# Query tiles in the planned order of the input norm and key/value tiles, context chunk first

## The chip, the cores and the metric

The kernel runs on one core of a Trainium2 chip. The metric is the time of one execution on the device in microseconds (us). One profiled execution gives the rows that are shown; its span runs from the first to the last instruction.

Engines by their names in the profile: PE (matrix products), PEld (its weight loads), DVE (vector), ACT (scalar, activations), POOL (GpSimd), SP (which issues nearly all DMAs). Each takes its instructions strictly in the order in which they were written for it; semaphores hold one back until its inputs are there.

## What is computed

One transformer layer over 2048 latent tokens of width 1024, with 256 context tokens ahead of them: a modulated norm, a combined input projection, softmax attention beside a gated delta rule, an output projection, and a gated MLP. What the change touches is the beginning:

```python
sh1, sc1, g1, sh2, sc2, g2 = ada_terms(c, w_mod[l], b_mod[l])
h = modulate(x, norm1_g[l], sh1, sc1)                  # latent tokens
hc = modulate(xc, norm1_g[l], cmod[0], cmod[1])        # context tokens
# of the columns of h @ w_in and hc @ w_in:
kc, vc = attn_kv(ck_a, cv_a, k_norm_g, None)
kl, vl = attn_kv(k_a, v_a, k_norm_g, rope)             # per-head norm, rotary
ql = attn_q(q_a, q_norm_g, rope)
o_attn = block_attention(ql, ...)
...
```

`modulate` is an RMS norm times (1 + scale) plus shift. `attn_q` and `attn_kv` normalise each head of 64, multiply by a gain and rotate by position.

## The kernel before

**The first stage.** The latent tokens come in four chunks of 512 (`x0` to `x3`, 8 tiles of 128x512 each), the context in one of 256 (called -1 in the names). The modulation's two parts are 64 small matmuls (`pm`), whose rows (`mrow`) are transposed into `mps`. A chunk's norm takes squares on ACT (`nsq`), added up on DVE and POOL (`nacc`), a sum over partitions on PE (`nps`), a reciprocal root on POOL (`nrc`), diagonals on DVE (`ndg`), and a matmul that spreads the result (`nrs`). `affine` multiplies each tile by scale and `nrs` on DVE, adds the shift on ACT into `hl..0` (the high part), and puts the rest into `hl..1` (the low part), on POOL for k = 0, 1, 2, 4 and on DVE otherwise. Context tiles are `hc`. High and low parts are kept for all four chunks in `hpool`, since the z projection and the delta rule's projections use them later.

**Key/value and query tiles.** For each 128 tokens `tokproj` makes 24 matmuls (`pq_kv`, 272 columns; `pq_q`, 256 columns, in two halves of four heads each, `q0` and `q1`). `headnorm` squares on ACT (`hsq`), sums on DVE and takes the reciprocal root on POOL (both `hss`), and multiplies on DVE (`hn`). `rope` has two products on POOL (`rb`) and two operations on DVE (`ra`), with a table per chunk (`t12k`, `t12q`) that POOL builds from a DMA. `put` splits into float16 parts (`st`, on ACT and DVE), transposes on PE (`pt`), copies on ACT (`qt`) and stores.

**What sets the order.** `Plan` records the instructions, estimates their durations, and lists them greedily: of those that could start next on an engine, the most urgent by its track's weight goes first. A track of kind "path" is urgent by the length of its remaining chain, one of kind "work" by how much of its PE work is left. The list is then issued as it stands. Before, the list held modulation (`mod`), key/value weights (`w`), norm (`x`) and key/value tiles (`kv`); the context chunk came last:

```python
for i in range(NCH):
    ...
    for k in range(KT):
        affine(i, x[k], rs, hl[i][0][:, k, :], hl[i][1][:, k, :], k)
    ...
x = load_x(-1)
...
plan.issue(dict(mod=("path", 30.0), w=("path", 20.0), kv=("path", KVW), x=("path", 1.0)))
```

The query tiles followed outside the list, through `Direct`, in the order of a loop over halves and tiles, with the transposes of `put` held back by three tiles (`later`, `run_later`); the z projection, also `Direct`, comes next. Weights of the query and z columns, squares, and input tiles that have no other place share the ring `x` of the pool `xp`, of 13 slots. Inputs 0 to 2 were loaded into `hpool` places of later chunks, input 3 into the ring.

Of the kernel before, what the change touches and what calls it, by code (L numbers as in the profile page):

```python
# [10 lines left out]
F32 = mybir.dt.float32  # L11
# [36 lines left out]
XB, LATER, KVW, DTB, PEC = 13, 3, 10.0, 5, 4.0  # L48
# [375 lines left out]

class Direct:
# [14 lines left out]
def kernel(  # L440
# [149 lines left out]
    later = []  # L590

    def run_later(keep):
        while len(later) > keep:
            later.pop(0)()

    def rope_table(e, wk, rows, nm, c, ro, sc):

        t12 = e.tile(wk, [P, 4, 2, 64], F32, "t12", f"t12{nm}{c}", 3)
        e.SY.dma_start(out=t12, in_=rope_d[:, 4 * c:4 * c + 4])
        gv = rows[:, ro:ro + 64]  # L600
        e.G.tensor_tensor(out=t12[:, :, 0, :], in0=t12[:, :, 0, :],
                        in1=gv.unsqueeze(1).broadcast_to([P, 4, 64]), op=ALU.mult)
        for hf in range(2):
            o = slice(32 * hf, 32 * hf + 32)
            oo = slice(32 - 32 * hf, 64 - 32 * hf)
            e.G.tensor_tensor(out=t12[:, :, 1, o], in0=t12[:, :, 1, o],
                            in1=gv[:, oo].unsqueeze(1).broadcast_to([P, 4, 32]), op=ALU.mult)
        if sc != 1.0:
            e.G.tensor_scalar(out=t12, in0=t12, scalar1=sc, scalar2=None, op0=ALU.mult)
        return t12  # L610
# [25 lines left out]
    def put(e, wk, a, nh, nm_, dst):  # L636

        st = e.tile(wk, [P, 4, 2, HD], F16, "st", f"st_{nm_}", 3)[:, :nh]
        e.S.copy(out=st[:, :, 0, :], in_=a)
        e.V.tensor_tensor(out=st[:, :, 1, :], in0=a, in1=st[:, :, 0, :], op=ALU.subtract)  # L640

        def fin():
            pt = e.tile(pst, [P, 1024], F16, "pt", f"pt_{nm_}", 2)
            with e.group():
                for h in range(nh):
                    e.PE.transpose(out=pt[:, h * P:(h + 1) * P], in_=st[:, h].rearrange("p a b -> p (a b)"), identity=id16)
            qt = e.tile(wk, [P, 4, P], F16, "qt16", f"qt_{nm_}", 2)[:, :nh]
            e.S.copy(out=qt, in_=pt[:, :nh * P].rearrange("p (h t) -> p h t", t=P))
            e.SY.dma_start(out=dst, in_=qt)
        later.append(fin)  # L650
        run_later(LATER)

    def front(plan, wk):
# [10 lines left out]
        xs = [place(2, 0, F32, "xs0"), place(3, 0, F32, "xs1"), place(3, 1, F32, "xs2")]  # L664
        hl = [[place(i, f, F32R, f"hl{i}{f}") for f in range(2)] for i in range(NCH)]
        firsts = hl[0] + wms + [xs[0], hl[2][1]] + xs[1:]
# [7 lines left out]
        def load_x(i):  # L674
            ts = []
            for k in range(KT):
                if 0 <= i < NCH - 1:
                    t = xs[i][:, k, :]
                elif i < 0:
# [3 lines left out]
                else:  # L683
                    t = mk(xp, [P, 512], F32, "x", f"x_{i}_{k}", XB)
# [34 lines left out]
        for nb in range(4):  # L719
            if nb == 2:  # L720
                x = load_x(0)
# [11 lines left out]
            row = mk(wk, [2, 512], F32, "qt", f"mrow_{nb}", 2)  # L733
# [4 lines left out]
        rs = stats(0, x)  # L738
# [52 lines left out]

        for i in range(NCH):
# [9 lines left out]
        x = load_x(-1)  # L802
        rs = stats(-1, x)
        hk = []
        for k in range(KT):
            t = mk(xp, [P, 2, TC], F32R, "x", f"hc_{k}", XB)
            affine(-1, x[k], rs, t[:, 0, :], t[:, 1, :], k)
            SY.dma_start(out=hcd[:, :, k, :], in_=t.bitcast(F32))
            hk.append(t)
        for cc in range(NCC):  # L810
            kv_tile(cc, lambda f, k, cc=cc: hk[k][:, f, cc * P:(cc + 1) * P], None)

        plan.track = "kv"
        run_later(0)
        plan.track = "x"
# [5 lines left out]
        return [[t.get() for t in h] for h in hl], ab.get(), rows.get(), gm.get(), sil.get(), [t.get() for t in wq]  # L821

    with tc.tile_pool(name="wk", bufs=2, reuse_waits="tile") as wk:
        hl, ab, rows, gm, sil, ws = front(Plan(tc, ps1, pst, psn), wk)


        direct = Direct(nc)

        def of_chunk(tt):
            sl = slice((tt % 4) * P, (tt % 4 + 1) * P)  # L830
            return lambda f, k: hl[tt // 4][f][:, k, sl]

        for hf in range(2):
            for tt in range(NTT):
                n_ = f"q{hf}_{tt}"
                if tt % 4 == 0:
                    t12 = rope_table(direct, wk, rows, f"q{hf}", tt // 4, R_Q, 0.125)
                ps = tokproj(direct, of_chunk(tt), ws, 256, n_)
                y = headnorm(direct, wk, ps[:, :256], 4, n_)
                a = rope(direct, wk, y, 4, tt % 4, t12, n_)  # L840
                put(direct, wk, a, 4, n_, qsc[tt, :, 4 * hf:4 * hf + 4, :])
            ws = load_w(direct, wiz[0] if hf else wiq[1], f"qz{hf}")
        run_later(0)
# [1587 lines left out]
```

## Time and profile before

| | |
|---|---|
| median of 3 runs | 3209.25 us |
| lowest, highest | 3205.55, 3211.18 us |
| the profiled execution | 3206.93 us |
| its span | 3205.2 us, mean granted PE clock 0.975 |
| busy over the span | PE 3049.6 (95%), PEld 1954.9 (61%), DVE 2387.5 (74%), ACT 1769.9 (55%), POOL 1532.4 (48%) |

PE's busy time counts matmuls that overlap and run slower at a low granted clock, so that 95% is no measure of what PE could do. Shares over the whole span mix stages with different limits; the stage in question is the first 268 us.

### The profile page before, as it was taken

To read this page: it belongs to the slowest core of one execution; us is meant where nothing else is said; L and a number is where in the kernel's file an instruction comes from. 1 tells how busy PE (TensorE), PEld (TensorE's weight loads), DVE (VectorE), ACT (ScalarE), POOL (GpSimd) and SP (SyncE) were. 2 spreads that over 40 slices of the span, in tenths; PEclk is the share of its full clock that TensorE was granted. 3 is DMA by queue.
4 is the path that set the end of the run, shared out by engine and by line. 5 is a ranking of instruction groups with operands and counts; after the bars stand their busy time and mean duration, and the time that the engine had idled before them with its cause. 6 is when DMAs were issued, how large, how long until landed. Compare 5 with 4: busy or idle time off the path is not lost.

```text
span 3205.2 us, 62953 instructions
## 1 busy us (share of the span) xinstructions
PE 3049.6 (95%) x25298; PEld 1954.9 (61%) x25298; DVE 2387.5 (74%) x3669; ACT 1769.9 (55%) x2876; POOL 1532.4 (48%) x1241
## 2 busy tenths in 40 slices
PE   6899999987999999999997999899999999999998
PEld 2789978874667777777775554344444444444445
DVE  5766487877777777788885778877777777976676
ACT  5534134445777777777776545555555555544332
POOL 4786365555887777777777434322333223000000
PEclk8899999997999999999998999999999999999999
DMA  6222334562112222233323565322222222696696
GB/s 246 86 77 82 113 128 127 168 177 81 49 42 76 67 78 84 93 117 110 104 96 114 216 236 187 122 92 99 92 99 99 93 96 79 204 309 203 218 311 216
DMA packets 287333, 423.63 MB, mean 132 GB/s; under 512 B 22984, under 2 KB 166952, under 8 KB 285744
## 3 DMA queue, kind: packets, MB, share of 16 engines
q1 hardware_dynamic: 285088, 414.19, 39.0%
q0 software_dynamic: 1952, 5.42, 0.6%
q8 instruction: 198, 3.24, 0.4%
q14 instruction: 95, 0.78, 0.1%
HBM read 284.15 MB, written 135.81 MB: 131 GB/s over the span
## 4 chain that ended last, share of the span: by engine, by line
PE 76%; DVE 10%; POOL 5%; DMA 3%; issue 3%; ACT 3%; SPq 0%; POOLq 0%; DVEq 0%; ACTq 0%
PE pdn L422 12%; PE ub L422 10%; PE sc L422 7%; PE uc L422 7%; PE ua L422 6%; PE ops L422 6%; PE po L422 6%; PE sm L422 3%; PE pa L422 2%; PE pg L547 1%; PE pg L546 1%; PE pg L548 1%; PE pw L422 1%; DVE mx L422 1%; PE pz L422 1%
## 5 line engine op out<-in xcount | busy, mean ns | idle before, releaser
L422 POOL TENSOR_TENSOR lp<-p,hp 128x1024 f16<-128x1024 f32 x288 | 620.0, 2160 | 208.5 <-DVE hp L422 84.0
L422 PEld LDWEIGHTS <-ws_u 128*128 128x128 f16 x3696 | 361.1, 98 | 444.4 <-issue 20.6
L422 DVE TENSOR_REDUCE mx<-sm 128x2 f32<-128x1024 f32 (+1 forms) x320 | 356.5, 1114 | 95.2 <-PE sm L422 92.3
L422 PE MATMUL pdn<-hid,wd 128*128 128x512 f16 (+1 forms) x1980 | 400.8, 365 | 0.0
L422 ACT ACTIVATE p<-sc 128x1024 f32<-128x1024 f32 x288 | 295.0, 1024 | 127.3 <-PE sc L422 123.6
L422 PEld LDWEIGHTS <-wd 128*128 128x128 f16 x1980 | 193.8, 98 | 204.7
L422 DVE SCALAR_TENSOR_TENSOR cv<-xa,ufw,cv 128x1025 f32<-128x1025 f32 (+1 forms) x176 | 254.9, 1501 | 48.8 <-ACT cv L422 48.7
L422 POOL TENSOR_TENSOR ws_u<-raw_u,ws_u 128x512 f16<-128x512 f32 x110 | 176.4, 1615 | 138.4 <-ACT ws_u L422 114.6
L422 PE MATMUL sc<-q,kh 128*128 128x512 f16 x576 | 220.4, 383 | 6.3 <-ACT p L422 5.9
L422 PE MATMUL sc<-qx,kx 128*128 128x512 f16 x576 | 220.1, 382 | 0.0
L422 POOL TENSOR_TENSOR nrc_f<-nrc_f,mhalf 128x8 f32<-128x8 f32 x3 | 5.5, 1837 | 424.1 <-DVE nrc_f L422 424.1
L422 ACT CAST hp<-p 128x1024 f16<-128x1024 f32 x192 | 201.0, 1047 | 3.7
L422 PE MATMUL ops<-vst,hp 128*128 128x65 f16 (+1 forms) x4608 | 191.9, 193 | 1.3 <-ACT hp L422 1.1
L422 PE MATMUL ua<-blk_a,ws_u 128*128 128x512 f16 x792 | 181.7, 379 | 1.9 <-ACT s L422 1.9
L422 PEld LDWEIGHTS <-hp 128*128 128x128 f16 x4608 | 164.9, 97 | 21.0 <-issue 7.1
L422 PE MATMUL po<-ol,ws_o 128*128 128x512 f16 x768 | 174.9, 385 | 0.1
L546 PE MATMUL pg<-hl,ws_g 128*128 128x512 f32 x384 | 152.7, 398 | 0.0
L548 PE MATMUL pg<-hl,ws_g 128*128 128x512 f32 x384 | 152.3, 397 | 0.0
L547 PE MATMUL pg<-hl,ws_g 128*128 128x512 f32 x384 | 151.7, 395 | 0.0
L422 POOL TENSOR_TENSOR usg<-usg,mhalf 128x3 f32<-128x3 f32 x22 | 19.1, 867 | 276.8 <-DVE usg L422 276.8
L422 ACT CAST t<-pa 128x512 f16<-128x512 f32 x216 | 124.5, 583 | 44.2 <-PE pa L422 40.3
L422 PE MATMUL sm<-kh,q 64*128 64x512 f16 (+1 forms) x320 | 119.0, 372 | 18.5 <-DVE mx L422 18.3
(704 smaller groups left out, 7779.3 us busy)
## 6 DMA issues: line engine op xcount, KB each, us to landing
rd<-in_wd SPq DMA_DIRECT2D x70, 512.0 KB
hid<-hidc SPq DMA_DIRECT2D x70, 512.0 KB
raw_u<-in_wu SPq DMA_DIRECT2D x44, 512.0 KB
tk<-gsc SPq DMA_DIRECT2D x34, 512.0 KB
tT<-gsc SPq DMA_DIRECT2D x66, 256.0 KB
hidc<-cv SPq DMA_DIRECT2D x22, 768.0 KB
wm<-in_wm SPq DMA_DIRECT2D x64, 256.0 KB
gsc<-kd SPq DMA_DIRECT2D x64, 256.0 KB
```

Source lines behind the costliest of these rows:

```text
L422: fn(**{k: v.get() if isinstance(v, Lazy) else v for k, v in kw.items()})
L546: PE.matmul(out=ps, lhsT=hi_l(k), rhs=hi_r(k), start=st, stop=False)
L547: PE.matmul(out=ps, lhsT=hi_l(k), rhs=lo_r(k), start=False, stop=False)
L548: PE.matmul(out=ps, lhsT=lo_l(k), rhs=hi_r(k), start=False, stop=en)
```

## The change

The query tiles become part of the planned list, as a track `q` of kind "work" with weight 0.5; key/value tiles become "work" with weight 2. The context chunk is normed first, then the four latent chunks. After each latent chunk's key/value tiles the list records that chunk's tiles of the first query half; the second half follows. The transposes of `put` are recorded at once, and the planner places them. Inputs 0, 2 and 3 land, tile by tile, in the places of their chunk's low parts (`places`, `Pieces`), and the affine's product goes to a ring tile `xm`. Input 1 lands where chunk 3's high part will be. The rope tables of keys and queries get rings of two each. The plan's fixed costs per instruction and its factor for DVE and POOL side by side (`fixed`, `PORT`) are set to the values that a later stage uses.

```diff
-XB, LATER, KVW, DTB, PEC = 13, 3, 10.0, 5, 4.0
+XB, QW, DTB, PEC = 13, 0.5, 5, 4.0
...
+class Pieces:
+    def __init__(self, tiles):
+        self.tiles = tiles
+    def __getitem__(self, idx):
+        return self.tiles[idx[1]][idx[0], idx[2]]
...
-        t12 = e.tile(wk, [P, 4, 2, 64], F32, "t12", f"t12{nm}{c}", 3)
+        t12 = e.tile(wk, [P, 4, 2, 64], F32, f"t12{nm[0]}", f"t12{nm}{c}", 2)
...
-        later.append(fin)
-        run_later(LATER)
+        fin()
...
-        xs = [place(2, 0, F32, "xs0"), place(3, 0, F32, "xs1"), place(3, 1, F32, "xs2")]
-        hl = [[place(i, f, F32R, f"hl{i}{f}") for f in range(2)] for i in range(NCH)]
+        def places(i, f, dtype, name):
+            return Pieces([mk(hpool, [P, 512], dtype, f"h{i}{f}{k}", f"{name}_{k}", 1) for k in range(KT)])
+        xs = [place(3, 0, F32, "xs1") if i == 1 else places(i, 1, F32, f"xs{i}") for i in range(NCH)]
+        hl = [[places(i, f, F32R, f"hl{i}{f}") if f and i != 1 else place(i, f, F32R, f"hl{i}{f}") for f in range(2)]
+              for i in range(NCH)]
...
-            V.scalar_tensor_tensor(out=x, in0=x, scalar=aff1[:, k, b:b + 1], in1=rs, op0=ALU.mult, op1=ALU.mult)
+            if i >= 0:
+                raw, x = x, mk(xp, [P, 512], F32, "x", f"xm_{i}_{k}", XB)
+            else:
+                raw = x
+            V.scalar_tensor_tensor(out=x, in0=raw, scalar=aff1[:, k, b:b + 1], in1=rs, op0=ALU.mult, op1=ALU.mult)
...
             if nb == 2:
-                x = load_x(0)
+                x = load_x(-1)
+            if nb == 3:
+                x0 = load_x(0)
...
-        rs = stats(0, x)
+        rs = stats(-1, x)
...
+        xn, hk = x0, []
+        for k in range(KT):
+            t = mk(xp, [P, 2, TC], F32R, "x", f"hc_{k}", XB)
+            affine(-1, x[k], rs, t[:, 0, :], t[:, 1, :], k)
...
+        x, rs = xn, stats(0, xn)
...
+        for cc in range(NCC):
+            kv_tile(cc, lambda f, k, cc=cc: hk[k][:, f, cc * P:(cc + 1) * P], None)
+        def q_tiles(hf, i, ws):
+            plan.track = "q"
+            t12 = rope_table(plan, wk, rows, f"q{hf}", i, R_Q, 0.125)
+            for tt in range(4 * i, 4 * i + 4):
+                n_ = f"q{hf}_{tt}"
+                ps = tokproj(plan, of_chunk(tt), ws, 256, n_)
+                y = headnorm(plan, wk, ps[:, :256], 4, n_)
+                a = rope(plan, wk, y, 4, tt % 4, t12, n_)
+                put(plan, wk, a, 4, n_, qsc[tt, :, 4 * hf:4 * hf + 4, :])
...
-        x = load_x(-1)
-        rs = stats(-1, x)
...
-        wq = load_w(plan, wiq[0], "q0")
-        plan.keep(wq)
+            if i == 0:
+                wq = load_w(plan, wiq[0], "q0")
+            q_tiles(0, i, wq)
+        wq = load_w(plan, wiq[1], "q1")
+        for i in range(NCH):
+            q_tiles(1, i, wq)
+        wz = load_w(plan, wiz[0], "z0")
+        plan.keep(wz)
...
-        plan.issue(dict(mod=("path", 30.0), w=("path", 20.0), kv=("path", KVW), x=("path", 1.0)))
+        plan.issue(dict(mod=("path", 30.0), w=("path", 20.0), kv=("work", 2.0), x=("path", 1.0), q=("work", QW)))
...
+        plan.fixed, plan.PORT = (150, 60, 0, 140, 42), 0.58
```

Before, PE has no query matmul ahead of the last key/value tile. The loops of the query and z tiles outside the list are gone for the queries and unchanged for z.

How the order moves, at three places. First ACT's rows around the last modulation row `mrow_3`. Before:

```order
L422 ACTIVATE nsq_a0_7_240<-xs0_122 128x512
L422 CAST ws_kv0_265<-raw_kv0_186 128x272
...
L422 COPY mrow_2_301<-pm_2_247 2x512
L422 ACTIVATE nacc_a1_307<-xs1_124 128x512
L422 COPY mrow_3_314<-pm_3_251 2x512
L422 ACTIVATE nsq_a1_1_320<-xs1_124 128x512
```

After:

```order
L422 ACTIVATE nacc_a-1_281<-xc_0_194 128x256
L422 COPY mrow_2_286<-pm_2_268 2x512
L422 CAST ws_kv0_290<-raw_kv0_211 128x272
...
L422 COPY mrow_3_307<-pm_3_271 2x512
L422 ACTIVATE nsq_a-1_1_311<-xc_0_194 128x256
```

Chunk 0's squares stood ahead of `mrow_3`, with those of chunk 1 behind it; now the context's squares but the first stand behind it, and chunk 0's behind those.

Second, POOL's rows where the first query tile stands. Before, behind the last key/value tiles (kv0 and kv1 are the context's):

```order
L422 TENSOR_TENSOR hss_kv1_1584<-hss_kv1_1584,mhalf_80 128x2
L601 TENSOR_TENSOR t12q02_2031<-t12q02_2031,rows_205 128x4x64
L606 TENSOR_TENSOR t12q02_2031<-t12q02_2031,rows_205 128x4x32 x2
L609 TENSOR_SCALAR t12q02_2031<-t12q02_2031 128x512
L496 TENSOR_SCALAR hss_q0_0_1676<-hss_q0_0_1676 128x4
L497 TENSOR_TENSOR hss_q0_0_1676<-hss_q0_0_1676,mhalf_80 128x4
```

After, among the key tables of chunk 2 and chunk 1's low parts (`hl11`):

```order
L422 TENSOR_TENSOR rb_kv5_882<-hn_kv5_870,t12k0_262 128x2x32 x2
L422 TENSOR_TENSOR t12k2_892<-t12k2_892,rows_224 128x4x64
L422 TENSOR_SCALAR hss_q0_0_940<-hss_q0_0_940 128x4
L422 TENSOR_TENSOR t12k2_892<-t12k2_892,rows_224 128x4x32
L422 TENSOR_TENSOR hss_q0_0_940<-hss_q0_0_940,mhalf_80 128x4
L422 TENSOR_TENSOR t12k2_892<-t12k2_892,rows_224 128x4x32
L422 TENSOR_SCALAR hss_q0_1_976<-hss_q0_1_976 128x4
L422 TENSOR_TENSOR hl11_992<-xm_1_0_886,hl10_903 128x512
```

The query tiles have moved from behind the norm into it.

Third, SP's loads. Before, the first query weights stand behind nearly all key/value stores and the context's stores (`hcd`):

```order
L422 DMA raw_q00_1523<-in_wiq 128x512
L422 DMA hcd_72<-hc_5_1504 256x1x256
...
L422 DMA ksc_62<-qt_kv17_1572 128x256
L422 DMA raw_q02_1582<-in_wiq 128x512
L599 DMA t12q02_2031<-in_rope 128x512
```

After, the rope tables stand behind the last input tile, and the query weights right behind the context's key/value stores:

```order
L422 DMA xs3_7_146<-in_xt 128x512
L422 DMA t12q00_258<-in_rope 128x512
L422 DMA t12q01_260<-in_rope 128x512
L422 DMA t12k0_262<-in_rope 128x512
...
L422 DMA vsc_63<-vs_kv1_556 128x128
L422 DMA raw_q00_589<-in_wiq 128x512
L422 DMA ksc_62<-qt_kv0_611 128x256
```

Tables moved behind all inputs, query weights ahead of the latent key/value tiles.

More of the change, by code (lines that the diff above doesn't have):

```diff
@@ L422, in issue, with get @@
                     fn(**{k: v.get() if isinstance(v, Lazy) else v for k, v in kw.items()})
+class Pieces:
[3 more added lines that the diff above has]
+        return self.tiles[idx[1]][idx[0], idx[2]]
+    def get(self):
+        return Pieces([t.get() for t in self.tiles])
 class Direct:
@@ L588, in tokproj @@
         return ps
[L590 to L594, printed above, removed]
     def rope_table(e, wk, rows, nm, c, ro, sc):
-        t12 = e.tile(wk, [P, 4, 2, 64], F32, "t12", f"t12{nm}{c}", 3)
+        t12 = e.tile(wk, [P, 4, 2, 64], F32, f"t12{nm[0]}", f"t12{nm}{c}", 2)
         e.SY.dma_start(out=t12, in_=rope_d[:, 4 * c:4 * c + 4])
@@ L663, in front @@
         wms = [place(1, f, F32, f"wms{f}") for f in range(2)]
-        xs = [place(2, 0, F32, "xs0"), place(3, 0, F32, "xs1"), place(3, 1, F32, "xs2")]
-        hl = [[place(i, f, F32R, f"hl{i}{f}") for f in range(2)] for i in range(NCH)]
-        firsts = hl[0] + wms + [xs[0], hl[2][1]] + xs[1:]
+        def places(i, f, dtype, name):
[3 more added lines that the diff above has]
+              for i in range(NCH)]
+        firsts = [hl[0][0]] + xs[0].tiles + wms + [hl[2][0]] + xs[2].tiles + [xs[1]] + xs[3].tiles
         ab = once(const, [P, NCK, 16], F32, "ab")
@@ L705, in affine @@
             hf = hi.bitcast(F32)
-            V.scalar_tensor_tensor(out=x, in0=x, scalar=aff1[:, k, b:b + 1], in1=rs, op0=ALU.mult, op1=ALU.mult)
+            if i >= 0:
+                raw, x = x, mk(xp, [P, 512], F32, "x", f"xm_{i}_{k}", XB)
+            else:
+                raw = x
+            V.scalar_tensor_tensor(out=x, in0=raw, scalar=aff1[:, k, b:b + 1], in1=rs, op0=ALU.mult, op1=ALU.mult)
             S.activation(out=hi, in_=x, func=AF.Identity, bias=mod1[:, k, b:b + 1])
@@ L732, in front @@
                               start=kp + k == 0, stop=kp + k == KT // 2)
-            row = mk(wk, [2, 512], F32, "qt", f"mrow_{nb}", 2)
+            row = mk(xp, [2, 512], F32, "x", f"mrow_{nb}", XB)
             S.copy(out=row, in_=pm[:2, :])
@@ L790, in of_chunk @@
             return lambda f, k: hl[i][f][:, k, sl]
+        xn, hk = x0, []
+        for k in range(KT):
+            t = mk(xp, [P, 2, TC], F32R, "x", f"hc_{k}", XB)
+            affine(-1, x[k], rs, t[:, 0, :], t[:, 1, :], k)
+            SY.dma_start(out=hcd[:, :, k, :], in_=t.bitcast(F32))
+            hk.append(t)
+        plan.track = "mod"
+        x, rs = xn, stats(0, xn)
+        plan.track = "x"
+        for cc in range(NCC):
[9 more added lines that the diff above has]
+                put(plan, wk, a, 4, n_, qsc[tt, :, 4 * hf:4 * hf + 4, :])
+            plan.track = "x"
         for i in range(NCH):
@@ L801, in front @@
                 kv_tile(NCC + 4 * i + j, of_chunk(4 * i + j), t12)
-        x = load_x(-1)
-        rs = stats(-1, x)
[L804 to L813, printed above, removed]
@@ L821, in front @@
-        return [[t.get() for t in h] for h in hl], ab.get(), rows.get(), gm.get(), sil.get(), [t.get() for t in wq]
+        plan.issue(dict(mod=("path", 30.0), w=("path", 20.0), kv=("work", 2.0), x=("path", 1.0), q=("work", QW)))
+        return [[t.get() for t in h] for h in hl], ab.get(), rows.get(), gm.get(), sil.get(), [t.get() for t in wz]
     with tc.tile_pool(name="wk", bufs=2, reuse_waits="tile") as wk:
-        hl, ab, rows, gm, sil, ws = front(Plan(tc, ps1, pst, psn), wk)
-        direct = Direct(nc)
@@ L829, in of_chunk @@
[L829 to L842, printed above, removed]
@@ L843, with of_chunk @@
-        run_later(0)
+        plan = Plan(tc, ps1, pst, psn)
+        plan.fixed, plan.PORT = (150, 60, 0, 140, 42), 0.58
+        hl, ab, rows, gm, sil, ws = front(plan, wk)
+    direct = Direct(nc)
+    def of_chunk(tt):
+        sl = slice((tt % 4) * P, (tt % 4 + 1) * P)
+        return lambda f, k: hl[tt // 4][f][:, k, sl]
     def decay_setup():
```

6 lines of the change are left out of this document (removed).

## The prediction

> **What bounds the kernel now.** The change touches the first stage alone, up to the point where the z projection starts, so I read that stage: first the busy times by stretch, then which tile opens the z stage, then who waits for whom, then the groups of the engine that is waited for. The stretches (time, length, then PE, PEld, DVE, ACT, POOL busy, the granted clock, the DMA share):
>
> ```profile
> core 0: us, PE busy (x) PEld busy (x) DVE busy (x) ACT busy (x) POOL busy (x), PEclk, DMA share, GB/s
> 0.00:44.00 44.00, 33.10 (x90) 7.84 (x90) 10.62 (x32) 13.37 (x26) 7.13 (x10) 1.00 0.96 339
> 44.00:100.00 56.00, 34.17 (x187) 29.20 (x188) 50.08 (x83) 39.15 (x83) 45.34 (x49) 0.72 0.32 110
> 100.00:154.00 54.00, 44.22 (x315) 40.93 (x314) 37.37 (x96) 28.16 (x93) 40.98 (x75) 0.91 0.27 78
> 154.00:170.00 16.00, 11.43 (x76) 10.55 (x76) 6.61 (x19) 5.89 (x19) 5.31 (x8) 0.89 0.51 147
> 170.00:214.00 44.00, 42.62 (x363) 41.76 (x364) 29.26 (x69) 16.36 (x39) 38.39 (x64) 0.96 0.22 63
> 214.00:268.00 54.00, 50.51 (x447) 49.11 (x446) 35.59 (x87) 22.90 (x56) 46.66 (x76) 1.00 0.22 69
> 268.00:321.50 53.50, 51.25 (x426) 50.63 (x425) 35.63 (x100) 24.99 (x47) 26.83 (x29) 0.97 0.31 98
> ...
> L585 PE MATMUL pq_z<-ws_qz,hl x128: 276/282/415, 268.3 to 321.3; 128*128 128x256 f32 x128
> ```
>
> The second row group says where the stage ends: the first z matmul starts at 268.3 us. Up to 268, POOL is busy 7.13 + 45.34 + 40.98 + 5.31 + 38.39 + 46.66 = 183.8 us, and 176.7 of the 224 us after 44 (79%). DVE has 158.9 of those 224 (71%), PE 183 (82%, but with stretched matmuls at a clock of 0.72 to 0.94). No engine is full over the whole, but each part has its own limit. From 44 to 100 (norm and key/value tiles) DVE is at 89% and POOL at 81%. From 100 to 154 nobody is over 82%. From 154 to 170 everything is half idle. From 170 on (query tiles) POOL is at (38.39 + 46.66)/98 = 87%. The waits, and two pieces of the chain that ended last, name the reasons:
>
> ```profile
> DVE hn_q L621 <- POOL hss_q L497: 10.9, 19, 1.6
> POOL t12q L601 <- DMA t12q<-in_rope: 10.7, 7, 5.0
> DVE ra_q L633 <- POOL rb_q L629: 9.5, 15, 1.6
> ...
> PE pq_q L585 <- DVE hn_q L621: 6.7, 6, 2.4
> PE pq_q L585 <- ACT ws_q L422: 4.5, 3, 2.0
> ...
> 154.63 4.09 DMA raw_q<-in_wiq
> 159.58 3.40 DMA raw_q<-in_wiq
> ```
>
> PE waits for `hn_q` (a PSUM buffer that DVE frees), which waits for POOL's `hss_q`: the query tiles go at POOL's pace. Around 160 the query weights have not come: two DMAs of 4.09 and 3.40 us are the chain. POOL's groups up to 275 us:
>
> ```profile
> L497 POOL TENSOR_TENSOR hss_q<-hss_q,mhalf 128x4 f32<-128x4 f32 x32 | 33.5, 1047 | 2.3
> L629 POOL TENSOR_TENSOR rb_q<-hn_q,t12q 128x128 f32<-128x128 f32 x64 | 32.0, 519 | 6.9 <-DVE hn_q L621 4.3 <-DVE ra_q L633 2.6
> ...
> L609 POOL TENSOR_SCALAR t12q<-t12q 128x512 f32<-128x512 f32 x8 | 12.4, 1554 | 0.6
> ...
> L496 POOL TENSOR_SCALAR hss_q<-hss_q 128x4 f32<-128x4 f32 x32 | 10.3, 322 | 8.1 <-DVE hss_q L618 5.5
> L606 POOL TENSOR_TENSOR t12q<-t12q,rows 128x128 f32<-128x128 f32 x16 | 8.7, 565 | 0.0
> ...
> L601 POOL TENSOR_TENSOR t12q<-t12q,rows 128x256 f32<-128x256 f32 x8 | 6.2, 772 | 10.7 <-DMA t12q<-in_rope 10.7
> ```
>
> The 32 query tiles cost POOL 33.5 + 32.0 + 12.4 + 10.3 + 8.7 + 6.2 = 103.1 us, 3.2 a tile. The change removes no part of it: POOL's rows stand in another order, but there are as many.
>
> **The change part by part.** The yardstick is therefore POOL's work against its share of the time. The new end of the stage is: the time at which the mixed work starts, plus POOL's work from there, divided by the share that it reaches.
>
> *Context first.* Before, the first latent chunk's sums were squared under the modulation matmuls, and its affine began right when the modulation was there. Now ACT has `mrow_3` ahead of the context's squares, so the sums start after it. The rows of before: when `mrow_3` and the affine came, and what the context's sums (`nacc_a-1`, with its four small matmuls), its rstd column (`nrc`, with two `ndg`) and its spread matmul cost, each filtered by its tile in a window:
>
> ```profile
> 40.73 0.56 ACT L422 COPY mrow<-pm 2x512 f32<-2x512 f32 x1
> 42.89 1.13 DVE L422 TENSOR_TENSOR aff<-aff,cols 128x16 f32<-128x16 f32 x1
> 44.05 2.72 DVE L422 SCALAR_TENSOR_TENSOR xs<-xs,aff,nrs_a 128x512 f32<-128x512 f32 x4
> ...
> 94.00:125.00 31.00, 0.67 (x4) 0.60 (x4) 1.95 (x4) 0.44 (x1) 2.26 (x3) 0.87 0.17 48
> ...
> 120.00:140.00 20.00, 0.72 (x3) 1.01 (x1) 0.83 0.17 47
> ...
> 120.00:140.00 20.00, 0.65 (x2) 0.30 (x2) 0.57 (x2) 0.83 0.17 47
> ```
>
> `mrow_3` ends at 40.73 + 0.56 = 41.3. One square of 0.4, then the chain of adds 1.95 + 2.26 = 4.2, the matmuls 0.67, rstd and diagonal 0.72 + 1.01 = 1.7, the spread 0.65: 48.6, where 44.05 stood. I take 48.5 (between 47, should handovers overlap, and 51, should each cost more). By then POOL has done 2.26 + 1.01 = 3.3 us instead of 7.13, so 183.8 - 3.3 = 180.5 us are left. The context's affine itself is not new, only earlier.
>
> *Inputs in the place of their low parts.* The same 32 multiplies write a ring tile instead of their own input, and as many DMAs go out: no instruction is added. Chunks 2 and 3 are now asked for at once, and the rope tables stand behind them on SP. Ahead of the tables are 16 loads of 512 KB, 24 + 8 of 256 KB (the latter by the rows below), the context (1 MB), key/value weights and rows (1.5 MB): 19.3 MB.
>
> ```profile
> wms<-in_wm SPq DMA_DIRECT2D x16, 512.0 KB
> xs<-in_xt SPq DMA_DIRECT2D x24, 256.0 KB
> x<-in_xt SPq DMA_DIRECT2D x8, 256.0 KB
> ```
>
> At the 339 GB/s of the first row that is 57 us; had all the time the best rate, it would be some 50. POOL comes to the tables at about 52, after the first chunk's sums: a wait of 0 to 5 us, I take 2. In return the later inputs (0.6 us of waiting now) and the query tables (10.7 us of POOL's waiting, the row above) are there early.
>
> *Query tiles in the plan.* POOL's holes are the gain: 56 + 54 - 86.3 = 23.7 us from 44 to 154, 10.7 from 154 to 170, 13 from 170 to 268. In the new order `hss_q`, `rb_q` and the tables stand between the norm's subtractions, and `raw_q00` stands ahead of the second key/value tiles, so the hole at 154 should go entirely. What share is reached? The first part (five affines, kv 0 to 13, q0_0 to q0_6) has both DVE and POOL heavily loaded; its bound from below is the 79% of POOL from 44 to 154, its best witness the 89% of DVE from 44 to 100. The second part (25 query tiles, four kv tiles) is like today's 170 to 268, 87%. I take 88% for the whole: 180.5/0.88 = 205.1.
>
> *The weights between halves, and the z stage.* The load of the second query half and of z stands in the same ring of 13; today's change of halves shows no stall at 214 (PE 50.51 of 54). From z on the code is the same; I cost it at nothing. Its cover is the PE work of 51.25 in 53.5 us; if late z weights broke it, the price is that of today's first weights, 16 - 11.43 = 4.6 us.
>
> **Sum.** 48.5 + 2 + 205.1 = 255.6, where 268.3 stood: -12.7 us. The profiled execution took 3206.93 us (span 3205.2), so 3194.2; the median of the runs shown, 3209.25, is 2.3 above it: 3196.5, said as 3196.
>
> PE does not forbid it:
>
> ```profile
> 250.00:268.00 18.00, 18.00 (x164) 17.73 (x162) 11.91 (x31) 7.87 (x19) 14.23 (x24) 1.00 0.15 49
> ```
>
> Here PE is full with 164 matmuls in 18 us, 0.11 each. The 432 of key/value, 768 of query and 164 transposes are 150 us, less than 205; PE would be at 73%.
>
> **The rivals.** *Port contention takes a good part back.* DVE and POOL lengthen each other when both stream from memory; the same four diagonals took 0.88 us with POOL idle and 4.42 beside POOL's sums and subtractions of 1.27 us each, and the subtractions of chunk 3 stretched too:
>
> ```profile
> 39.05 0.88 DVE L422 TENSOR_SCALAR ndg_a<-k,nrc_a 128x128 f32<-128x128 f32 x4
> 57.60 4.42 DVE L422 TENSOR_SCALAR ndg_a<-k,nrc_a 128x128 f32<-128x128 f32 x4 [0.72 <-POOL nrc_a L422]
> 57.54 1.27 POOL L422 TENSOR_TENSOR nacc_a<-nacc_a,nsq_a 128x512 f32<-128x512 f32 x1
> ...
> L422 DVE SCALAR_TENSOR_TENSOR hl<-x,mod,hl x4: 740/1420/1749, 120.2 to 124.0; 128x512 fp32r<-128x512 f32 x4
> L422 POOL TENSOR_TENSOR hl<-x,hl x4: 1252/1297/1803, 115.2 to 124.0; 128x512 fp32r<-128x512 f32 x4
> ```
>
> The Trainium skill, GPSIMD Engine Reference, section Specifications, says that GpSimd's memory interfaces are shared with VectorE and contend with its instructions that have two tensor inputs or run in a two-port mode. The trace agrees with these rows, and by that rule a denser mix costs more per instruction. Its price here: if 36 affine operations of three chunks stretch like the four (1.42 for 0.74), DVE gains 36 x 0.68 = 24 us, to 158.9 + 24 = 183; at the 89% that is its best, 206, which alone changes nothing; POOL's two-input work of some 45 us stretching by a tenth adds 4.5/0.88 = 5, and uneven queues behind stretched instructions about as much: stage end 262 to 265, time 3203 to 3206.
>
> *PE-like packing.* The planner's order fits, POOL reaches 95%: 50.5 + 190 = 240.5, time 3181. For it speaks that 32 independent tiles now fill any hole; against it that no stretch above shows POOL over 87%.
>
> *Slower: the in-order queues keep POOL at the share of the planned stage.* Every engine takes its rows in the planned order, and the planned part of today reached 86.3/110 = 78% although the order was planned too. Query and key/value tiles share one `rb`, two `hn`, and five free slots of the ring of 13 while eight hold query weights; one late row holds up all behind it. At 78%: 50.5 + 231 = 282, time 3223. It decides from a share of 180.5/(268.3 - 50.5) = 83% downwards; there the late start is no longer earned back.
>
> *The change does nothing measurable:* the share lies at 82 to 86%, between today's planned and query parts, so that the filled holes pay only for the late start; stage end 260 to 270, time 3199 to 3209.
>
> **How the numbers follow.** Forecast (share 86 to 91%) 0.40, contention 0.17, close packing 0.15, nothing measurable 0.10, slower 0.18. The range holds shares from 81% (50.5 + 223 = 273.5, time 3214) to 95.5% (3180). Measurement tells 0.2%, 6.4 us, from no change: faster means under 3202.8, slower over 3215.7. Forecast and packing are faster (0.55); contention straddles 3203, two fifths of it faster (0.07) and three fifths the same (0.10), with all of the case of nothing (0.10); of the slower rival two thirds lie beyond 3215.7 (0.12), the rest within (0.06). That gives 0.62 faster, 0.26 same, 0.12 slower.
>
> **What would show it.** The first z matmul at about 255 instead of 268.3; POOL at 86 to 91% from 50 to there; the first context affine at 48 to 49; no wait for `raw_q` and none of several us for the rope tables; from the first z matmul to the end the same 2937 us. I am wrong if POOL's operations get longer by over a tenth, if DVE or ACT shows waits for ring tiles (`xm`, `rb`, `hn`) in the first part, if PE starves at either change of weights, or if the z stage lasts longer.

## The result, and the profile after

The changed kernel takes 3226.9 us (median of 4 runs, 3221.8 to 3228.9) where the kernel before takes 3209.7 in the same runs: ratio 1.0052, interval [1.004, 1.0065]. It is slower by 17 us. Forecast were 3196 us and a gain of 13; the sign was wrong, and the time lies above the range.

The profiled execution has a span of 3225.7 us (3205.2 before). The same stretches as before (time, length, busy times of PE, PEld, DVE, ACT, POOL with counts, granted clock, DMA share, GB/s), and the row that ends the stage:

```profile
0.00:44.00 44.00, 31.25 (x80) 6.74 (x80) 6.63 (x23) 10.40 (x23) 1.75 (x7) 0.97 0.95 341
44.00:100.00 56.00, 38.46 (x183) 32.60 (x184) 40.26 (x78) 28.94 (x74) 37.23 (x47) 0.66 0.49 168
100.00:154.00 54.00, 45.36 (x307) 41.15 (x305) 37.98 (x80) 30.96 (x71) 41.99 (x61) 0.87 0.14 40
154.00:170.00 16.00, 11.47 (x60) 9.96 (x61) 14.14 (x22) 7.37 (x19) 14.29 (x17) 0.68 0.06 17
170.00:214.00 44.00, 38.28 (x313) 36.84 (x312) 31.92 (x77) 22.48 (x58) 33.87 (x55) 0.96 0.21 62
214.00:268.00 54.00, 49.82 (x428) 47.79 (x427) 33.56 (x83) 22.20 (x59) 46.28 (x76) 1.00 0.25 75
...
188.00:281.40 93.40, 84.90 (x721) 82.37 (x722) 60.67 (x152) 39.09 (x104) 78.30 (x130) 0.98 0.24 72
```

```profile
L598 PE MATMUL pq_z<-ws_z,hl x256: 277/281/420, 281.4 to 383.4; 128*128 128x256 f32 x128
```

The first z matmul comes at 281.4 us instead of 268.3: 13.1 of the 20.4 us by which the last matmul is later (3212.3 against 3191.9) arise in the stage that was changed. The hole from 154 to 170 is gone, as intended: POOL has 14.29 us of 16 there, 5.31 before. But up to 100 us POOL has done 39.0 us of work where it had done 52.5. Both stages whole, as one row each (before, then after):

```profile
0.00:268.30 268.30, 216.36 (x1479) 179.65 (x1479) 169.82 (x384) 125.96 (x315) 184.03 (x279) 0.91 0.39 127
```

```profile
0.00:281.40 281.40, 227.49 (x1479) 187.72 (x1480) 173.54 (x384) 128.06 (x315) 186.12 (x279) 0.88 0.36 122
```

The instructions are as many (1479, 384, 315, 279), POOL's busy time grew by 2 us, and PE needs 11.1 us more for the same 1479 matmul records, at a granted clock of 0.88 instead of 0.91. DVE's, ACT's and POOL's busy times grew by 2 to 4 us; for the rest of the 13 us these three wait. Pieces of the chain that ended last, from the changed kernel (pieces called issue, of less than 0.1 us each, are left out): the start, and a stretch in which query tiles stand between the norm's subtractions:

```profile
35.10 4.78 DMA rows<-in_rows
39.90 0.22 DVE gm L422
...
47.44 1.86 DVE ws_kv L422 x2
49.30 1.41 DVE ndg_a-1_379 L422 x2
50.76 1.24 PE nrs_a-1_383 L422 x2
52.02 0.87 DVE xc L422 x2
...
111.06 0.98 POOL hss_q L422
112.06 0.43 DVE hn_q L422
112.53 0.43 POOL hss_q L422
113.04 1.33 POOL hl L422
114.37 0.42 POOL rb_q L422
114.79 0.97 POOL hss_q L422
```

At the start the context's affine (`xc`) comes at 52.0. In the second stretch read the starts: from one `hss_q` power to the next 3.73 us pass (111.06 to 114.79). Within them a query tile's `hn_q` can only follow its own power; then come the next tile's scaling (112.53), a subtraction of 1.33 us and an `rb_q`, and only behind these two the next tile's power. POOL is nearly full in this stretch (4.84 us of the 5 from 110 to 115), so it shows who stands behind whom, and not where POOL's idle time lies. The waits from 44 us to the stage's end (us in total, times, longest):

```profile
...
DVE hn_q L422 <- POOL hss_q L422: 20.1, 24, 2.5
...
POOL hss_kv L422 <- DVE hss_kv L422: 10.6, 5, 8.3
...
PE pq_kv L422 <- DVE hn_q L422: 6.5, 4, 4.9
POOL t12k L422 <- DMA t12k<-in_rope: 6.3, 2, 3.2
```

`hn_q` waits 20.1 us for POOL where it waited 10.9 before. POOL's own longest wait, 8.3 us up to 93.15, is of another kind: it waits for the sum of a key/value tile, and the chain there is mostly key/value matmuls, at a granted clock of 0.55 from 85 to 90 us:

```profile
85.41 5.21 PE pq_kv L422 x25
90.62 0.12 PE nps_a L422 x2
90.73 1.63 PE pq_kv L422 x12
```

### The profile page after: what moved, and what is told of

It is laid out like the page before. It is cut to its first block, busy times and chain, and to the rows that moved or that the text cites. A ratio compares the mean times of both kernels' runs of the same rounds, so it can differ in the third digit from the quotient of the medians.

```text
span 3225.7 us, 62936 instructions
## 1 busy us (share of the span) xinstructions
PE 3061.8 (95%) x25298; PEld 1964.2 (61%) x25298; DVE 2392.6 (74%) x3669; ACT 1772.0 (55%) x2876; POOL 1532.9 (48%) x1241
## 4 chain that ended last, share of the span: by engine, by line
PE 75%; DVE 10%; POOL 5%; issue 4%; DMA 3%; ACT 3%; SPq 0%; POOLq 0%; DVEq 0%; ACTq 0%
PE pdn L422 12%; PE ub L422 10%; PE sc L422 7%; PE uc L422 7%; PE ua L422 6%; PE ops L422 6%; PE po L422 6%; PE sm L422 3%; PE pa L422 2%; DVE mx L422 1%; DMA wm<-in_wm 1%; PE pw L422 1%; PE pg L560 1%; PE pg L559 1%; PE pg L561 1%
```

## The experiments

Each with the median, the ratio to the kernel before in the same runs (which took 3209.65 to 3211.93) and the first z matmul of the profiled execution. That last figure is of one execution; in `early_il` (3229.5 us) and `interleave` (3230.5) it was the longest of the runs, some 9 and 4 us above the median:

| kernel | us | ratio [interval] | first z |
|---|---|---|---|
| changed | 3226.9 | 1.0052 [1.004, 1.0065] | 281.4 |
| ctx_last | 3239.9 | 1.0088 [1.007, 1.0106] | 295.0 |
| q_outside | 3233.7 | 1.0072 [1.0055, 1.0089] | 290.8 |
| both_back | 3251.3 | 1.0124 [1.0109, 1.0139] | 305.1 |
| old_costs | 3226.5 | 1.0046 [1.0031, 1.0061] | 281.8 |
| stats_track | 3231.6 | 1.0063 [1.0047, 1.008] | 285.1 |
| before_places | 3225.4 | 1.0047 [1.0032, 1.0062] | 284.9 |
| before_places_track | 3219.5 | 1.0028 [1.0019, 1.0038] | 280.0 |
| kv_path | 3230.9 | 1.0061 [1.0046, 1.0076] | 283.1 |
| interleave | 3226.6 | 1.0047 [1.0033, 1.0062] | 280.1 |
| early_il | 3220.9 | 1.0034 [1.0021, 1.0047] | 282.0 |
| before_places_il | 3233.5 | 1.0068 [1.0051, 1.0084] | 292.3 |
| before_kv | 3217.4 | 1.0016 [1.0007, 1.0026] | 271.9 |
| warm | 3230.4 | 1.0054 [1.0039, 1.0069] | 284.8 |
| before_warm | 3214.5 | 1.0009 [0.9999, 1.0018] | 273.9 |
| less_pe | 3224.1 | 1.0042 [1.0027, 1.0056] | 275.0 |
| less_pool | 3214.1 | 1.001 [1.0001, 1.0019] | 269.1 |
| before_scale | 3204.2 | 0.9974 [0.9962, 0.9985] | 261.0 |
| early_scale | 3213.8 | 1.0007 [0.9998, 1.0015] | 266.4 |

**Which part loses? Parts taken back one at a time.** `ctx_last` loads and computes the context after the last chunk again:

```
-            if nb == 2:  x = load_x(-1)
-            if nb == 3:  x0 = load_x(0)
+            if nb == 2:  x = load_x(0)
...
+        x = load_x(-1); rs = stats(-1, x); ...      # behind the chunks
         wq = load_w(plan, wiq[1], "q1")
```

> The changed kernel with the context chunk normed last again (chunk 0's sums under the modulation, as before); query tiles stay in the planned list, inputs and planner costs stay as changed. Theory A (the context-first order is the loss: the first latent affine came at 65.95 us instead of 44.05, and the work behind it was not denser): the first latent affine is back at 44 to 46 and the first z matmul comes at 262 to 268, time 3203 to 3212. Theory B (the mixing of query tiles into the norm is the loss, the start is made up for): first z matmul at 278 or later, time over 3221.

`q_outside` takes the query tiles out of the planned list:

```
-            q_tiles(0, i, wq)
...
+        for hf in range(2):
+            for tt in range(NTT): ...               # directly, as before
```

> The changed kernel with the query tiles behind the planned list again, as before (with their held-back transposes); context first, inputs and planner costs as changed. Theory A: the late start stays and nothing fills the holes, so the first z matmul comes at 280 or later, time 3222 to 3235. Theory B: the norm runs undisturbed, the stage ends at 270 to 275, time 3210 to 3216.

`both_back` does both, so that of the change only the inputs' places with the product tile `xm`, the modulation rows in ring x, the planner's numbers, the key/value track's weight and transposes, and the two rings of rope tables are left:

> Context last and query tiles outside: only the inputs' places (with the ring tile of the affine's product) and the planner's costs and key/value weight are as changed. Theories A and B both: within 4 us of the kernel before, 3206 to 3214, first z matmul 266 to 272. A rival (the places or the costs are the loss): 3220 or more.

`old_costs` is the changed kernel with the planner's numbers of before (`plan.fixed` and `plan.PORT` not set):

> The changed kernel with the planner's fixed costs and its factor for DVE beside POOL as before; all else changed. A and B: 3221 to 3232, the costs move single rows only. Rival C (the new cost values make a worse list): 3215 or less.

Theory A fails in `ctx_last`, B in `q_outside`, both in `both_back`, and C in `old_costs` (the numbers of B in `ctx_last` and of A in `q_outside` did come, but neither theory has both); what came in `both_back` is the rival, that the places or the costs are the loss (3220 or more). Undoing the context's place or the query tiles' makes it slower, so each of these two named parts is a gain: from `both_back` 17.6 us for the context, 11.4 for the query tiles, 24.4 for both. The planner's numbers do nothing in the changed kernel that can be told. What loses is the rest: `both_back` stands 41 us behind the kernel before.

**The inputs' places and the turns in ring x.** A ring's buffers are given in the order of recording within a track. The squares of chunk i+1 (`nsq_a`) and the eight products of chunk i (`xm`) now stand in ring x on one track, the squares behind the products. The squares in before, and after:

```profile
L422 ACT ACTIVATE nsq_a<-xs x21: 612/614/631, 18.3 to 53.7; 128x512 f32<-128x512 f32 x21
L422 ACT ACTIVATE nsq_a<-x x7: 627/630/633, 61.3 to 78.9; 128x512 f32<-128x512 f32 x7
```

```profile
L422 ACT ACTIVATE nsq_a<-xs x28: 612/629/655, 41.6 to 162.9; 128x512 f32<-128x512 f32 x28
```

The last square came at 78.9 and now comes at 162.9, ahead of chunk 3's affine. That it costs time was the next theory (D). Four kernels: `stats_track` (the changed kernel, squares and sums of chunks 1 to 3 on a track of their own, `n`, of kind "path" with weight 1),

```
         def stats(i, x):
+            was = plan.track
+            if i > 0: plan.track = "n"
...
+            plan.track = was
```

> The changed kernel with one thing undone in effect: the statistics of chunks 1 to 3 are recorded on a track of their own, so that their squares need not take their turn in ring x behind the eight product tiles (xm) that the affine now allocates there. Nothing else changes. Theory D (the products' new ring tiles hold the next chunk's squares back, so that each chunk's chain becomes serial): chunk 1's squares start at 41 to 55 us instead of 71, chunk 3's rstd comes by 125 instead of 177.5 us, first z matmul at 250 to 266 us instead of 281.4, time 3194 to 3212 against 3226.9. Rival E (the weight of the key/value track, work 2.0, is the loss): first z within 3 us of 281, time 3222 to 3230. Rival F (the inputs' pieces or the separate rope-table ring land late): the same as E.

`before_places` (the kernel before with the places and `xm` alone: the lines on `xs`, `hl`, `firsts` and the multiply of the diff above),

> The kernel before with one part of the change alone: inputs land in tiles of their own where the low parts go, and the affine writes a product tile in ring x instead of working in place. Context last, query tiles outside, weights, costs and rope-table ring as before. Theory D: the chunks' chain becomes serial, first z at 283 to 300 us against 268.3, time 3224 to 3243. Rivals E and F in its rope-table form: nothing of theirs is in this kernel, so 3206 to 3213. F in its pieces form: slower as in D, and no better in the next run.

`before_places_track` (the two edits together),

> The kernel before with the inputs' places and product tiles, as in the run ahead of it, and the statistics of chunks 1 to 3 on a track of their own. Theory D: back to about the kernel before, first z 262 to 275 us, 3203 to 3216. F in its pieces form: within 5 us of the run ahead of it.

and `kv_path`:

```
-kv=("work", 2.0)
+kv=("path", 10.0)
```

> The changed kernel with the key/value track's weight put back from work 2.0 to path 10.0; the rings' turns stay. Rival E: first z at 260 to 270 us and 3205 to 3214. Theory D: chunk 3's rstd stays after 165 us, first z at 278 to 290, time 3222 to 3236.

The places with the product tile alone cost 14.7 us (3225.4 against 3210.7), though they add no instruction; that is shown. Theory D holds for a part at most: with the own track the kernel before gets 5.9 of them back, which the intervals hardly tell apart, and the changed kernel nothing. In the latter the last square comes at 79.9 instead of 162.9, but the products come late:

```profile
L422 DVE SCALAR_TENSOR_TENSOR xm<-xs,aff,nrs_a x32: 730/737/748, 85.2 to 155.3; 128x512 f32<-128x512 f32 x32
```

The first starts at 85.2 us (65.9 in the changed kernel), the last at 155.3 (186.3): on a track of their own the sums of chunks 1 and 2 ran ahead of the first products, and DVE did them first. So in this kernel early squares did not bring the stage's end forward (285.1 against 281.4). In `before_places` a single wait at the change to the query tiles has grown too (5.5 us before):

```profile
POOL hss_q L509 <- DVE hss_q L631: 12.2, 1, 12.2
```

The weight (`kv_path`) is not the loss: 3230.9.

**The turns again, with nothing else moved.** `interleave` records square and sum k of the next chunk right behind affine k, on the same track:

```
+            by = stats_by(i + 1, xn)
             for k in range(KT):
                 affine(i, x[k], rs, ...)
+                rn = next(by, None)
-                x, rs = xn, stats(i + 1, xn)
```

> The changed kernel with one order of recording altered: square and sum k of the next chunk are recorded right after affine k of this one, on the same track, instead of after all eight. No weight, place or instruction differs; only the turns in ring x do. Theory D2 (the turns behind the products cost, and an own track fails because it lets the squares run ahead of the context's products as well): first z at 262 to 275 us instead of 281.4, time 3206 to 3220 against 3226.9. Rival G (the turns are harmless; the loss is the late start by 100 us and then POOL's share in the mixed order, which is PE, DVE and POOL waiting for each other's short tiles): first z within 4 us of 281, 3221 to 3232.

`early_il` also records the context's sums ahead of `mrow_3`:

```
             if nb == 3:
                 x0 = load_x(0)
+                rs = stats(-1, x)
```

> As the run ahead of it, and the context's squares and sums are recorded ahead of the fourth row of the modulation (mrow_3), so that they don't take their ring turn behind it. Theory D2: the first context affine comes at 44 to 47 us instead of 52.0, and the stage ends 4 to 8 us before that of the run ahead of it: 3200 to 3214. Rival G: the same gain of 4 to 8 us, but from 281: 3218 to 3226. If the early start is eaten by a later wait: no difference to the run ahead of it.

`before_places_il` is `before_places` with the same interleaving:

> The kernel before with the inputs' places and product tiles (3225.4), and the squares of the next chunk recorded between the affines of this one. Theory D2: 3207 to 3216 and first z at 266 to 276 us instead of 284.9. Rival G: 3221 to 3230.

`before_kv` is the kernel before with the weight and the transposes of the change alone:

```
-        later.append(fin); run_later(LATER)
+        fin()                                       # in the plan
-kv=("path", KVW)
+kv=("work", 2.0)
```

> The kernel before with two small parts of the change alone: the key/value track's weight is work 2.0 instead of path 10.0, and the transposes of a planned key/value tile are recorded with it instead of three tiles later. Places, context and query tiles as before. Theory D2: these parts cost little by themselves, 3205 to 3216. Rival E2 (they are the 26 us that lie between the kernel with the places alone, 3225.4, and the one with context and query tiles back, 3251.3): 3225 to 3240, first z at 283 to 298 us.

Interleaving gives nothing in the changed kernel (3226.6) and loses 8 us in `before_places`. It is a weak test of theory D, since in these two kernels the last square moved little (from 162.9 to 156.2, and from 109.7 to 105.9); with the own track, where the squares did come early, the stage still ended at 285.1 and 280.0. So D is not borne out as the main cause. `before_kv` costs 6 us, so of the 26 us between `before_places` and `both_back` that part is small. If the parts add up, 14.7 of the 41 us go with the places, 6 with the weight and the transposes, and some 20 are left. They go with the first square: with the modulation's rows moved into ring x and the context last, the first chunk's squares stand behind `mrow_3`. ACT's rows of `both_back` at `mrow_3`; then the squares and products of `before_places`, and those of `both_back`:

```profile
37.95 0.57 ACT L422 COPY mrow<-pm 2x512 f32<-2x512 f32 x1 [0.28 <-PE pm L422]
38.44 3.74 ACT L422 ACTIVATE nsq_a<-xs 128x512 f32<-128x512 f32 x7
```

```profile
L422 ACT ACTIVATE nsq_a<-xs x28: 611/621/637, 17.6 to 109.7; 128x512 f32<-128x512 f32 x28
L422 DVE SCALAR_TENSOR_TENSOR xm<-xs,aff,nrs_a x32: 732/734/748, 41.8 to 136.9; 128x512 f32<-128x512 f32 x32
```

```profile
L422 ACT ACTIVATE nsq_a<-xs x28: 612/614/624, 38.4 to 129.8; 128x512 f32<-128x512 f32 x28
L422 DVE SCALAR_TENSOR_TENSOR xm<-xs,aff,nrs_a x32: 737/740/748, 57.6 to 156.0; 128x512 f32<-128x512 f32 x32
```

The first square comes 20.8 us later, the first product 15.8, the stage's end 20.2. The two kernels differ in the weight, the transposes, the planner's numbers and the rope rings as well, so the link from the start to the end is argued, not shown by itself: no run puts the modulation's rows back alone, or the rope rings. In the changed kernel it is the context's shorter squares that stand in that turn; recording them early (`early_il`) brought the affine only from 52.0 to 51.4. There DVE sat idle for `rows` up to 40.89 us and prepared them ahead of the context's last sums, as in the `DMA rows` and `gm` pieces of the chain above. The median of `early_il` is 6 us below that of the changed kernel, with intervals that overlap; what it gained is not explained.

**What is the bound? Clock, PE, POOL.** `warm` is the changed kernel in its order, with filler matmuls ahead of the sums and of the rstd spread:

```
+    FILL_NPS = {'a-1': 8, 'a0': 2, 'a1': 3, 'a2': 3, 'a3': 3}
+    FILL_NRS = {'a-1': 8, 'a0': 3, 'a1': 4, 'a2': 4, 'a3': 4}
+            e.PE.matmul(out=ps[:, 256:512], lhsT=ident, rhs=k32[:, 0:256], start=True, stop=True)
```

> The changed kernel, in the same order, with 45 filler matmuls (f32, 128x256 of a constant, into unused columns of the sums' PSUM tile) that PE runs while it would wait: 8 ahead of the context's sums and 8 ahead of its rstd spread, 2 to 4 at those of each chunk. Theory H (PE's low granted clock after idle gaps is what the changed stage lost: the same 1483 matmuls take 227.5 us instead of 216.4): clock from 44 to 100 us above 0.8 instead of 0.66, the other matmuls 8 to 12 us shorter in sum, first z at 270 to 277 instead of 281.4, time 3213 to 3223. Rival G (the pace is POOL's and the chains' over it; a slow PE only fills its idle time): the clock rises, first z within 3 us of 281, 3222 to 3233.

`before_warm` is its control:

> The kernel before with fillers of the same kind: 3 ahead of the sums of chunks 1 to 3, 8, 6 and 4 ahead of their rstd spreads, 3 ahead of the context's. It is the control: under theory H as a cause of the difference it gains less than the changed kernel, 0 to 5 us (3205 to 3213); if both gain alike, the clock costs time but does not explain the difference. Rival G: no gain.

`less_pe` does without the third matmul of each group:

```
                 e.PE.matmul(out=ps[:, :n], lhsT=h(0, k), rhs=ws[k][:, 1, :], ...)
-                e.PE.matmul(out=ps[:, :n], lhsT=h(1, k), rhs=ws[k][:, 0, :], ...)   # in the plan
```

> The changed kernel, planned as it is, but the third of the three matmuls of each eighth of a planned key/value or query tile is left out (the low part of the input times the weights): 400 matmuls fewer, some 45 us of PE at 0.11 each. If PE is the bound of the mixed stage: first z at 235 to 250 us, time 3178 to 3196. Rival G (POOL is the bound): first z at 272 to 282, 3215 to 3230. If no engine is, and chains of short waits are: in between, 255 to 270.

`less_pool` does without the power (the scaling stays, with other constants):

```
-        rsqrt_pool(ss, ss, nh, 1.0 / HD, G=e.G)
+        e.G.tensor_scalar(out=ss, in0=ss, scalar1=1e-6, scalar2=0.01, op0=ALU.mult, op1=ALU.add)
+        e.G.tensor_tensor(out=ss, in0=ss, in1=mhalf.broadcast_to([P, nh]), op=ALU.mult)
```

> The changed kernel, planned as it is, but POOL's power in the norm of each planned key/value or query tile (18 of 0.70 and 32 of 1.03 us) is replaced by a multiplication, so the norms are not the reference's; some 35 to 40 us less of POOL's 184.5, and as much off the chain of each tile. Rival G (POOL is the bound): first z at 235 to 250 us, time 3178 to 3196. PE as the bound: first z at 272 to 282, 3215 to 3230. Chains of short waits: in between, 255 to 270.

The rows of `warm` (two stretches, the stage whole, the fillers), of `less_pe` and of `less_pool`:

```profile
44.00:100.00 56.00, 43.35 (x207) 37.53 (x207) 39.34 (x74) 28.72 (x73) 36.80 (x46) 0.76 0.49 167
100.00:154.00 54.00, 45.64 (x335) 40.77 (x335) 39.13 (x85) 31.09 (x72) 41.93 (x62) 1.00 0.15 41
0.00:284.80 284.80, 240.65 (x1563) 198.69 (x1564) 172.72 (x384) 127.43 (x315) 185.68 (x279) 0.92 0.36 120
...
L424 PE MATMUL nps_a<-k 128*128 128x256 f32 x52 | 14.5, 422 | 0.0
...
L424 PE MATMUL nps_a-1_357<-k 128*128 128x256 f32 x32 | 10.4, 497 | 0.3 <-DVE nrc_a-1_372 L424 0.3
```

```profile
0.00:275.00 275.00, 185.04 (x1079) 143.14 (x1080) 172.14 (x383) 126.36 (x315) 184.24 (x277) 0.83 0.37 124
```

```profile
0.00:269.10 269.10, 220.75 (x1478) 183.28 (x1479) 173.96 (x385) 126.32 (x315) 152.31 (x279) 0.90 0.39 127
```

The fillers (42 of them; the profile has 84 records, 24.9 us) lifted the clock from 0.66 to 0.76 and from 0.87 to 1.00. All other matmuls together then took 215.7 us instead of 227.5 (216.4 in the kernel before), and the stage ended no earlier (284.8); the control gained nothing either (3214.5). So the longer matmuls by themselves do not make the loss; whether the fillers held something else up was not separated. Without 400 matmuls PE is busy 42.5 us less, and the stage ends 6.4 us earlier; the time (1.0042) cannot be told from the changed kernel's. Without the powers POOL is busy 33.8 us less, and the stage ends 12.3 us earlier. Had either engine been the bound, nearly all of its saved work would have come back; so neither is. `less_pool` came out where "chains of short waits" had it (255 to 270); `less_pe`, at 275.0, in the range for POOL as the bound, which `less_pool` then rules out. More of the chain goes through POOL than through PE; that this is because POOL's power lies between a tile's sum and its norm fits, but `less_pool` shortens POOL's work and each tile's chain at once. DVE, busy 173.5 of the 281.4 us, was not lightened in any run.

**What a handover is worth.** The scaling ahead of that power goes from POOL to VectorE, behind VectorE's own sum. `before_scale` does it in the kernel before, `early_scale` in `early_il`:

```
-        rsqrt_pool(ss, ss, nh, 1.0 / HD, G=e.G)
+        e.V.tensor_scalar(out=ss, in0=ss, scalar1=1.0 / HD, scalar2=EPS, op0=ALU.mult, op1=ALU.add)
+        e.G.tensor_tensor(out=ss, in0=ss, in1=mhalf.broadcast_to([P, nh]), op=ALU.pow)
```

> The kernel before, but the scaling ahead of the power in each head norm (POOL, 18 of 0.25 and 32 of 0.32 us, 14.8 us in all) is done by VectorE, right behind its own sum. Theory I (chains of short handovers set the pace; less_pool gave 12.3 us for 34 us of POOL's work): 3 to 6 us earlier, 3204 to 3209. If POOL's work were the bound, 14.8/0.79 = 19 us earlier, 3192. If VectorE's queue eats it: 3209 to 3216.

> The kernel that records the squares between the affines and the context's sums early (3220.9), with the same scaling on VectorE. Theory I: 3 to 8 us earlier, 3212 to 3219, more than in the kernel before since there the query tile's norm waits 20 us in all for POOL instead of 11. It would stay behind the kernel before.

`before_scale` takes 3204.2 us, ratio 0.9974 [0.9962, 0.9985]: a version that beats both kernels, if by a quarter of a per cent. Its stage ends at 261.0, 7.3 us earlier for 15.6 us less of POOL's busy time (168.4 instead of 184.0). In `early_scale` the median is 7.1 us below that of `early_il`, and cannot be told from the kernel before. How long `hn_q` waits for POOL, in `early_il`, in `early_scale` and in `before_scale`:

```profile
DVE hn_q L422 <- POOL hss_q L422: 19.3, 24, 2.7
```

```profile
DVE hn_q L422 <- POOL hss_q L422: 7.2, 18, 0.9
```

```profile
DVE hn_q L622 <- POOL hss_q L620: 12.7, 19, 1.8
```

In the mixed order this wait falls to less than half, and the stage ends 15.6 us earlier (282.0 to 266.4; but the profiled execution of `early_il` was the longest of its runs). In `before_scale` the wait did not fall (12.7 us, 10.9 before), so there the gain does not come by it, and what it comes by was not traced. Once that handover is shorter, the mixed stage is as short as that of the kernel before, 266.4 against 268.3; but against `before_scale`, with the same scaling and a stage of 261.0, it is still 5.4 us longer. The time is not yet below that of the kernel before: from the first z matmul to the end of the span it is 2947.6 us there, 2944.3 in the changed kernel and 2936.9 before. Of the 7.4 us between the changed kernel and the one before, 2.6 lie between the first z and the first gate matmul (`pg`; 102.4 against 99.8 us). Where the others come from was not tried and stays open.

## Why the prediction was wrong

*The yardstick.* The sum took POOL's work and divided it by a share, 180.5/0.88 = 205.1. This is the step that failed. POOL's work was right: from 50.5 us to the stage's end it did 180.0 us. But that took 230.9 us, a share of 78%, and the 25.8 us by which the stage ended later than forecast (281.4 against 255.6) lie in this term; up to 3.5 of them belong to the later start, below. It assumes that POOL is the bound and that more independent tiles fill its holes. `less_pool` refutes it: 33.8 us less at the share of 0.78 that POOL really had from 44 us on (184.4 of 237.4) would have been 43 us, and it was 12.3. A share is an outcome of the waits here, not a property of an engine. The measured shares by part: 74% from 44 to 188, where norm, key/value and query tiles are mixed (186.12 - 1.75 - 78.30 = 106.1 of 144), and 84% from 188 on (78.30 of 93.40). For the second part the forecast's witness (87%) was nearly right. The first came out below even the 79% that the forecast had taken as its bound from below. Its "best witness", DVE's 89% from 44 to 100, was another engine's share in another order; in the changed kernel DVE itself has 40.26 of these 56 us, 72%.

*The slower rival* had the number (78%, end 282, time 3223; measured 281.4 and 3227) and a mechanism that is right in kind: every engine takes its rows in order, and a short step waits behind a long one, as the chain's 3.73 us per query tile and the 20.1 us of `hn_q` show. It had 0.18. That the total agrees is in part luck: the 78% is a mean of 74 and 84, this rival has no term for the places, and taking out the mixing that it blames made the kernel slower, by 6.9 us (`q_outside`). What it named in particular, shared buffers of `rb` and `hn`, was not tried; the largest waits that can be for a buffer are 6.5 us (PE's `pq_kv` for `hn_q`, above) and 5.0 (`xm` for `hl`):

```profile
DVE xm L422 <- POOL hl L422: 5.0, 5, 1.5
```

*"No instruction is added"* held, and was taken for the price. The inputs' places were costed at nothing but their loads. `before_places` measured 14.7 us. What is costed by its instructions alone misses what a new ring tile does to the order. Turns account for 5.9 us of it by `before_places_track`; how the rest comes about is not settled.

*Parts that were not costed at all.* The move of the modulation's rows into ring x stood in the diff and has no term of its own; the sum took squares behind `mrow_3` as given, in the context's start. With the context last it goes with a first product 15.8 us later (`both_back`).

*The start.* 48.5 us forecast, bounds 47 to 51, measured 52.0. The spread and the diagonals were longer than their rows of before (1.24 and 1.41 us against 0.65 and 0.57), and `ws_kv` of 1.86 stood ahead of them on DVE. The size was off by 3.5 us.

*What held.* The context first and the query tiles in the plan are gains, 24.4 us together as measured from `both_back`; the hole at 154 is gone. Nothing of this was enough for the price of the rest. The rope tables waited (6.3 us for `t12k`, I took 2) and the query tables nearly not at all (1.9 instead of 10.7).

*Contention* is not borne out as the explanation. The Trainium skill (GPSIMD Engine Reference, section Specifications) says that GpSimd shares its memory interfaces with VectorE and contends with its instructions that have two tensor inputs or run in a two-port mode. That could have made POOL's operations longer in the denser mix. Here the subtractions of low parts are not longer (before, then after):

```profile
L422 POOL TENSOR_TENSOR hl<-x,hl x4: 1252/1297/1803, 115.2 to 124.0; 128x512 fp32r<-128x512 f32 x4
```

```profile
L422 POOL TENSOR_TENSOR hl<-xm,hl x16: 1263/1292/1451, 69.9 to 186.2; 128x512 fp32r<-128x512 f32 x16
```

POOL's sum grew by 2.1 us in all, by the two rows of the stage, and DVE's by 3.7.

*"From z on the code is the same; I cost it at nothing"* was short by 7.4 us in the profiled executions.

## What to carry to other kernels

An engine at 80% in a stage with several such engines is not yet a bound: before dividing its work by a share, ask which row each of its idle stretches waits for, and follow one tile's handovers through the queues. Mixing more independent work into an in-order list fills holes, but short steps then stand behind longer ones. Giving VectorE the scaling of its own sum gave more than other turns, a warmer clock or 400 fewer matmuls did. And a diff is costed by what it does to the order in every ring it touches, also where no instruction is added.

## What was not expected of the hardware

The granted clock is 0.50 in four rows of 5 us on end, although PE is nearly full in one of them. The changed kernel's rows:

```profile
45.00:50.00 5.00, 1.01 (x4) 0.93 (x4) 3.33 (x5) 2.52 (x5) 3.27 (x3) 0.50 1.05 389
50.00:55.00 5.00, 2.04 (x4) 1.00 (x4) 3.65 (x8) 2.38 (x6) 1.44 (x2) 0.50 1.05 379
55.00:60.00 5.00, 4.88 (x20) 4.62 (x21) 4.01 (x9) 2.21 (x6) 3.48 (x5) 0.50 1.06 380
60.00:65.00 5.00, 3.65 (x14) 2.82 (x13) 3.99 (x8) 1.47 (x4) 5.00 (x6) 0.50 0.68 233
...
100.00:105.00 5.00, 5.00 (x41) 4.38 (x40) 4.11 (x12) 2.73 (x8) 2.07 (x6) 1.00 0.24 66
```

Twenty matmuls fill 4.88 us at 0.50, twice as long each as the 41 at 1.00. It would have been easy to take the 11 us of longer matmuls for nearly the whole loss of 13; in `warm` the matmuls other than the fillers took 11.7 us less, and the stage ended no earlier.
